# Token block sums: the sum of a quarter's high and low part made once a round and subtracted as one tile

## The chip, the cores and the metric

The kernel runs on one core of a Trainium2 chip. The metric is the device time of one execution in microseconds (us); the time of a kernel is the median of several executions.

## The reference

One decoder block on 1024 tokens of width 1024, all in float32, in two halves. What the change touches is the very front of it: the normed tokens `h` and their product with `w_in`.

```python
h = rmsnorm(x, g_mix_norm[l])
proj = jnp.einsum('bsd,de->bse', h, w_in[l])
sb_q, sb_k, sb_v, fx_q, fx_k, fx_v, f_logit, m_q, gate_logit = split_columns(proj, SPLITS)
# three attention branches (stick-breaking, forgetting, memory), gated and merged
mh = rmsnorm(mem, g_mem_norm[l])
mkv = jnp.einsum('bmd,de->bme', mh, w_mem_kv[l])
# ... x = x + merged @ w_out, then a squared-ReLU MLP with w_ff_up and w_ff_down
```

## The kernel before, in words

Every product is made on TensorE (PE) from a *high* part (rounded to a reduced 32-bit format, fp32r) and a *low* part (the rest) of both operands, three matmuls for one: high by high, high by low, low by high. So an operand that comes as one float32 tile has to be split: ScalarE (ACT) copies it to the high part, VectorE (DVE) subtracts this from the tile and writes the low part. Both steps stand in the helper `split`, and nearly all of them show in a profile as L1149 (ACT) and L1150 (DVE).

The large products are not made block by block but by a scheme with seven products, P1 to P7, for four blocks. P5, P6 and P7 need sums of blocks of the tokens. `h` turned, with its 1024 features on the partitions, lies in `hTh` (high) and `hTl` (low); a *quarter* is four chunks of 128 features by 512 tokens. The generator `sums_T` makes three sums out of three quarters, one chunk k a round, four rounds: with h11 the first quarter (it is kept only as high and low part, `b11`), t1 and t2 the same chunk of the two quarters of the second 512 tokens, which come back by DMA from a DRAM copy (`h_scr`) as float32,

- t1 = t1 - h11, the operand of P5
- t2 = t2 - t1, the operand of P6
- w_ = t2 - h11, the operand of P7

and each is then split into its place in `T_of` by `both`. Since h11 exists as two parts only, each subtraction of it takes two DVE instructions in a row, one for the high, one for the low part (L628 and L629, L635 and L636). L632 is t2 - t1. Those instructions run between 66.7 and 92.2 us of the profiled execution. The places t1, t2 and w_ are taken from a rotation `SN` of ten tiles of 128x512, which the first-stage evictions (L1328 on ACT, L1332 on DVE, values; L1753, gates) and the stores behind them use as well.

In the same stretch PE works through the first products: values of the forgetting branch (into `fn` go the forget logits, L1360), one gate block, then keys and values of the memory, `w_kv`. The weights of `w_kv` come in eight pieces of 512 KB through SP's DMA queue into two raw tiles, `ra` and `rb`, in turn, and are split into pairs of high and low tiles: (`ha`, `la`), (`hc`, `lc`), (`hb`, `lb`), again in turn. A piece's transfer can only be issued once the split of the piece before it in the same raw tile is over on DVE, and after whatever stands in front of it in SP's queue.

The order of the work is not the chip's choice. A planner inside the kernel (`Machine`) runs all generators against assumed costs (`dve_time` and the like), and each engine's instructions are written out in the order in which this plan begins them. On the chip every engine then takes its own queue strictly in that order. A changed cost or an instruction more or less can therefore move the order on every engine. All engines wait for each other by semaphores, and a tile out of a rotation can be written only after its last reader.

Of the kernel before, what the change touches and what calls it, by code (L numbers as in the profile page):

```python
# [18 lines left out]
ALU = mybir.AluOpType  # L19
# [19 lines left out]
def f32(ap):  # L39
    return ap.bitcast(F32)  # L40
# [3 lines left out]
def tile_hybrid_block(  # L44
# [23 lines left out]
    nc = tc.nc  # L68
# [120 lines left out]
    class Machine:  # L189
# [12 lines left out]
        def spawn(self, gen, late=0.0):  # L202

            done = Event()
            proc = [gen, late, done, None]
            self.at(self.now, lambda: self.resume(proc, None))
            return done
# [90 lines left out]
    def dve_time(*cols):  # L298
        return sum(0.08 + 0.00105 * m for m in cols)
# [60 lines left out]
    def tiles(pool, tag, n, shape, dt=F32):  # L360
        return Places([pool.t(tag, [P, shape], dt) for _ in range(n)])
# [3 lines left out]
    SN, RS, S1 = tiles(E, "sn", 10, 512), tiles(R, "raw", 4, 1024), R.t("s1", [P, 4, 256])  # L365
# [210 lines left out]
    def prologue():  # L576

        keys = [[("x", s)] for s in range(ST)] + [[("m", 0), ("m", 1)]]
        xs = [("x", s) for s in range(2, PLAIN)] + [(k_, s) for s in range(PLAIN, ST) for k_ in ("x", "xt")]
        spawn(fetch_tokens([("x", 0), ("g", "x"), ("x", 1), ("w", 0), ("w", 1), *xs[:1], ("g", "xt"), *xs[1:], ("g", "mt"),  # L580
                            *[(k_, s) for s in range(2) for k_ in ("m", "mt")]]))
        spawn(warm(half_made[2, 1]), 100.0)
        evs = [spawn(norm(ks_, 4.0 * i - 8.0, half_made[AFTER[i]] if i in AFTER else None), 4.0 * i - 8.0)
               for i, ks_ in enumerate(keys)]
        for ev in evs:
            yield ev
        spawn(small_loads())
        N.close()
        T = Pool("t", h=6)
        holder["T"] = T  # L590
        for kind in ("P5", "P6", "P7"):
            T_of[kind] = tuple(T.t("h", [P, 4, 512], F32R) for _ in range(2))
        spawn(sums_T(), 6.0)
# [10 lines left out]
    def second_half(k):  # L604

        t1, t2 = yield Get(SN, 2)

        def issue():
            nc.sync.dma_start(t1, h_scr[:, k, :])
            nc.sync.dma_start(t2, h_scr[:, 4 + k, :])  # L610
        yield from transfer(issue, 2 * P * 2048, 0.2)
        fetched_h[k] = t1, t2
    fetched_h = {}

    def sums_T():
        for s in range(4, ST):
            yield h_kept[s]
        coming = spawn(second_half(0))
        for k in range(4):
            b11 = tuple(t[:, k, 0:512] for t in (hTh, hTl))  # L620
            yield coming
            t1, t2 = fetched_h[k]
            if k < 3:
                coming = spawn(second_half(k + 1))
            w_ = yield Get(SN)

            def first():
                nc.vector.tensor_tensor(t1, t1, f32(b11[0]), ALU.subtract)  # L628
                nc.vector.tensor_tensor(t1, t1, f32(b11[1]), ALU.subtract)  # L629

            def second():
                nc.vector.tensor_tensor(t2, t2, t1, ALU.subtract)  # L632

            def third():
                nc.vector.tensor_tensor(w_, t2, f32(b11[0]), ALU.subtract)  # L635
                nc.vector.tensor_tensor(w_, w_, f32(b11[1]), ALU.subtract)  # L636
            yield Op("DVE", dve_time(512, 512), first)
            yield Op("DVE", dve_time(512), second)
            two = [spawn(both("P6", k, t2)), spawn(both("P5", k, t1), 2.0)]
            yield Op("DVE", dve_time(512, 512), third)  # L640
            two.append(spawn(both("P7", k, w_), 1.0))
            for ev in two:
                yield ev
            SN.put(t1, t2, w_)
        yield kv_over
        MT.close()
        holder["T4"] = T4 = Pool("t4", side="right", h=2)
        T_of["P4"] = tuple(T4.t("h", [P, 4, 512], F32R) for _ in range(2))
        for k in range(4):
            b21 = tuple(t[:, 4 + k, 0:512] for t in (hTh, hTl))  # L650
            t2 = tuple(t[:, k] for t in T_of["P6"])
            t4, w_ = yield Get(SN, 2)

            def fourth():
                nc.vector.tensor_tensor(t4, f32(b21[0]), f32(t2[0]), ALU.subtract)
                nc.vector.tensor_tensor(w_, f32(b21[1]), f32(t2[1]), ALU.subtract)
                nc.vector.tensor_tensor(t4, t4, w_, ALU.add)
            yield Op("DVE", dve_time(512, 512, 512), fourth)
            yield spawn(both("P4", k, t4))
            SN.put(t4, w_)  # L660

    def both(kind, k, raw):
        hi, lo = (t[:, k] for t in T_of[kind])
        yield from split(hi, lo, raw)
        machine.fire(T_made[kind][k])
# [1496 lines left out]
    with tc.manual_schedule():  # L2162
# [256 lines left out]
        def turn_half(s, k4):  # L2419
# [17 lines left out]
            if s >= 4:  # L2437
                yield turned[s - 4]
                if k4:
                    yield t1_made[s]  # L2440
                to = (t1raw, t2raw)[k4]

                def sums_T():
                    for h in range(2):
                        k2 = slice(2 * h, 2 * h + 2)
                        tt(to[h][:, :, cs], tr4[:, k2, :], t1raw[h][:, :, cs] if k4 else traw[:, k2, cs], ALU.subtract)
                yield Op("DVE", dve_time(256, 256), sums_T)
                if k4 == 0:
                    machine.fire(t1_made[s])
# [139 lines left out]
        first = {}  # L2589
# [266 lines left out]
```

## Time and profile before

| | us |
|---|---|
| median of 3 runs (lowest, highest) | 1657.71 (1656.91 to 1659.15) |
| the profiled execution's own time | 1657.59 |
| its span, from the first to the last instruction | 1655.8 |
| PE busy in the span | 1646.7 |
| DVE busy in the span | 1293.4 |
| ACT busy in the span | 849.5 |
| granted TensorE clock, mean | 0.999 |

Around the span lie 1657.59 - 1655.8 = 1.8 us. Of the views used below, the one of waits says which engine's instruction stood still for which other engine's, in total, how often, and the longest; the chain of waits goes back from the last instruction, at each step to what released it; the timeline gives start, duration and, in brackets, the idle time ahead of an instruction and its releaser; windows give busy time in a stretch. A matmul's end is modelled, so two matmuls' starts say more than their durations.

### The profile page before, as it was taken

What the parts mean: (1) busy time and instruction counts of PE and PEld (TensorE: products, weight loads), DVE (VectorE), ACT (ScalarE), POOL (GpSimd) and SP (SyncE); (2) the same over time, 40 slices, a digit from 0 to 9 for tenths busy, and PEclk for the clock granted to TensorE, in tenths of its full rate; (3) what the DMA queues carried; (4) which work ended last, traced back from release to release, by engine and by line L of the source; (5) the groups of instructions that cost most, each with busy time, mean ns of one, the idle gap of its engine ahead of it and who ended that gap; (6) DMA issues with size and microseconds to landing.
All of it is one profiled execution on the core that took longest, in us unless ns stands there. A gap on an engine that the chain in (4) does not pass through costs nothing.

```text
span 1655.8 us, 25062 instructions
## 1 busy us (share of the span) xinstructions
PE 1646.7 (99%) x9082; PEld 1429.4 (86%) x9082; DVE 1293.4 (78%) x2123; ACT 849.5 (51%) x1476; POOL 254.8 (15%) x440
## 2 busy tenths in 40 slices
PE   9999999999999999999999999999999999999999
PEld 8988899998888988888888888888888888888887
DVE  7798789955549888868877798987777777788875
ACT  6355555535458898977772465533233345233331
POOL 0000000000153232245400011021221120000000
PEclk9999999999999999999999999999999999999999
DMA  9846655568474455477866762154444475564532
GB/s 331 254 142 200 213 165 187 169 183 252 146 245 137 150 155 169 138 222 223 219 167 216 256 231 98 52 178 146 156 156 153 146 285 198 193 215 158 203 127 76
DMA packets 153629, 302.68 MB, mean 183 GB/s; under 512 B 18081, under 2 KB 58593, under 8 KB 153122
## 3 DMA queue, kind: packets, MB, share of 16 engines
q1 hardware_dynamic: 121970, 201.45, 36.2%
q0 software_dynamic: 31536, 99.64, 19.6%
q8 instruction: 71, 1.16, 0.3%
q14 instruction: 52, 0.43, 0.1%
HBM read 201.89 MB, written 99.13 MB: 182 GB/s over the span
## 4 chain that ended last, share of the span: by engine, by line
PE 94%; DVE 3%; DMA 2%; ACT 1%; issue 0%; SPq 0%
PE pp L1551 11%; PE pp L1239 9%; PE pp L2101 9%; PE pp L2791 8%; PE sc L1551 7%; PE sc L1239 6%; PE sc L2101 5%; PE tr L2791 4%; PE sc L2791 4%; PE tr L1012 4%; PE pv L1551 3%; PE pv L2791 3%; PE sc L1029 2%; PE tr L2101 2%; PE pp L1029 2%; PE pp L2346 2%
## 5 line engine op out<-in xcount | busy, mean ns | idle before, releaser
L1019 DVE TENSOR_TENSOR ptl<-tr,pth 128x512 fp32r<-128x512 f32 (+1 forms) x160 | 99.1, 628 | 25.5 <-ACT pth L1017 24.5
L2101 PE MATMUL pp<-h,oh 128*128 128x512 f32 x384 | 118.3, 389 | 0.0
L1017 ACT ACTIVATE pth<-tr 128x512 fp32r<-128x512 f32 (+1 forms) x160 | 87.5, 557 | 33.5 <-PE sc L1029 13.9
L2189 ACT ACTIVATE cu<-pp 128x512 f32<-128x512 f32 x48 | 28.7, 598 | 137.3 <-PE pp L2101 137.3
L2101 PEld LDWEIGHTS pp<-h,oh 128*128 128x128 f32 x384 | 72.0, 188 | 15.0 <-ACT oh L2532 0.2
L1468 POOL DMA_DIRECT2D raw<-w_in x32 | 24.2, 757 | 393.3 <-DVE lc L1150 205.2
L2101 PE MATMUL pp<-h,ol 128*128 128x512 f32 x192 | 74.9, 390 | 0.5 <-DVE ol L2037 0.5
L938 DVE TENSOR_TENSOR_SCAN e<-r,e 128x384 f32<-128x384 f32 (+3 forms) x64 | 66.3, 1044 | 6.8 <-ACT e L923 6.4
L2791 PE MATMUL pp<-h,h 128*128 128x512 f32 x288 | 66.6, 389 | 0.0
L2791 PE MATMUL pp<-sop,sop 128*128 128x512 f32 x288 | 66.6, 389 | 0.0
L2791 PEld LDWEIGHTS pp<-h,h 128*128 128x128 f32 x288 | 54.1, 188 | 11.2
L2791 PEld LDWEIGHTS pp<-sop,sop 128*128 128x128 f32 x288 | 54.1, 188 | 11.2
L1012 PE MATMUL tr<-ident,e 128*128 128x128 f32 x416 | 62.5, 273 | 0.0
L1012 PEld LDWEIGHTS tr<-ident,e 128*128 128x128 f32 x416 | 50.5, 140 | 9.9
L2118 POOL DMA_DIRECT2D s_scr<-cu x48 | 26.1, 544 | 189.3 <-DVE cu L2108 179.8
L1029 PE MATMUL sc<-pth,v 128*128 128x256 f32 (+1 forms) x174 | 48.0, 298 | 0.0
L2037 DVE TENSOR_TENSOR cu<-cu,sc 128x512 f32<-128x512 f32 x33 | 22.5, 682 | 32.5 <-ACT cu L2189 32.5
L1099 POOL DMA_DIRECT2D h<-sbk_scr x64 | 33.3, 527 | 94.1 <-PE pv L156 29.5
L2706 ACT ACTIVATE h<-t 128x2048 fp32r<-128x2048 f32 (+1 forms) x9 | 15.4, 1724 | 59.5 <-DVE t L2037 55.4
L2037 DVE TENSOR_TENSOR x<-x,pp 128x512 f32<-128x512 f32 x39 | 26.6, 683 | 22.8 <-PE pp L2791 22.8
L2101 PEld LDWEIGHTS pp<-h,ol 128*128 128x128 f32 x192 | 36.0, 188 | 8.7 <-DVE ol L2037 1.2
L2118 POOL DMA_DIRECT2D s_scr<-s x60 | 32.5, 542 | 71.0 <-DVE s L2037 64.4
(797 smaller groups left out, 5546.7 us busy)
## 6 DMA issues: line engine op xcount, KB each, us to landing
ur<-s_scr SPq DMA_DIRECT2D x26, 1024.0 KB
raw<-w_in POOLq DMA_DIRECT2D x32, 512.0 KB, 5.2
raw<-w_up SPq DMA_DIRECT2D x60, 256.0 KB
s_scr<-s POOLq DMA_DIRECT2D x60, 256.0 KB, 2.5
g<-w_down SPq DMA_DIRECT2D x14, 1024.0 KB
s_scr<-cu POOLq DMA_DIRECT2D x48, 256.0 KB, 2.3
h<-sbk_scr POOLq DMA_DIRECT2D x64, 128.0 KB, 3.1
o<-gate_scr SPq DMA_DIRECT2D x32, 256.0 KB
```

The source lines that it names most:

```text
L938: nc.vector.tensor_tensor_scan(out=back, data0=rho[:, :u][:, ::-1], data1=back, initial=0.0 if last else beta[:, c + u:c + u + 1], op0=ALU ...
L1012: nc.tensor.transpose(tr[:, jj * 256 + a * P:jj * 256 + (a + 1) * P], es[a][:, j * P:(j + 1) * P], ident)
L1017: yield Op("ACT", act_time(512 - lo_c), lambda: nc.scalar.activation(ph[:, lo_c:], tr[:, lo_c:], AF.Copy))
L1019: yield Op("DVE", dve_time(512 - lo_c), lambda: nc.vector.tensor_tensor(pl[:, lo_c:], tr[:, lo_c:], f32(ph[:, lo_c:]), ALU.subtract))
L1029: nc.tensor.matmul(pv[0][:, c_:256], pair.v[:, j, b, :], p_[:, jj * 256 + c_:(jj + 1) * 256], start=(k == 0 and n_ == 0 and i == 0), stop= ...
L1099: nc.gpsimd.dma_start(f32(t[k][rows_, :]), src)
L1239: nc.tensor.matmul(ps, a_, b_, start=(first and i == 0), stop=(last and i == n - 1))
L1551: nc.tensor.matmul(out_, a_, b_, start=(first and n == 0 and j == 0), stop=(last and n == 3 and j == len(todo) - 1), skip_group_check=True)
L2037: nc.vector.tensor_tensor(out_, a_, b_, op)
L2101: nc.tensor.matmul(ps, w[a_][:, k * P:(k + 1) * P], h[b_][k], start=(first and k == 0 and i == 0), stop=(last and k == 3 and i == 2), skip ...
L2118: nc.gpsimd.dma_start(s_scr[r0:r0 + P, :], t)
L2791: nc.tensor.matmul(ps, a_[:, c, qs], b_[:, c, :], start=(kind in ("P1", "P2", "P7") and c == 0 and i == 0), stop=(kind in ("P2", "P4", "P3 ...
```

## The change

In each round the two parts of h11 are added into w_ first, before the round waits for t1 and t2. Both subtractions of h11 then take w_ as one tile, and the last one writes over it. L622 is the new addition; L629, L632 and L635 are the three subtractions in the changed file. The planner is told of one DVE instruction instead of two at either place, and of the new one. The place w_ is taken ahead of the wait for t1 and t2 instead of behind it.

```diff
         for k in range(4):
             b11 = tuple(t[:, k, 0:512] for t in (hTh, hTl))
+            w_ = yield Get(SN)
+            yield Op("DVE", dve_time(512), lambda: nc.vector.tensor_tensor(w_, f32(b11[0]), f32(b11[1]), ALU.add))
             yield coming
             t1, t2 = fetched_h[k]
             if k < 3:
                 coming = spawn(second_half(k + 1))
-            w_ = yield Get(SN)
 
             def first():
-                nc.vector.tensor_tensor(t1, t1, f32(b11[0]), ALU.subtract)
-                nc.vector.tensor_tensor(t1, t1, f32(b11[1]), ALU.subtract)
+                nc.vector.tensor_tensor(t1, t1, w_, ALU.subtract)
 
             def second():
                 nc.vector.tensor_tensor(t2, t2, t1, ALU.subtract)
 
             def third():
-                nc.vector.tensor_tensor(w_, t2, f32(b11[0]), ALU.subtract)
-                nc.vector.tensor_tensor(w_, w_, f32(b11[1]), ALU.subtract)
-            yield Op("DVE", dve_time(512, 512), first)
+                nc.vector.tensor_tensor(w_, t2, w_, ALU.subtract)
+            yield Op("DVE", dve_time(512), first)
             yield Op("DVE", dve_time(512), second)
             two = [spawn(both("P6", k, t2)), spawn(both("P5", k, t1), 2.0)]
-            yield Op("DVE", dve_time(512, 512), third)
+            yield Op("DVE", dve_time(512), third)
             two.append(spawn(both("P7", k, w_), 1.0))
```

The order that results: PE (8750 rows), POOL and SP have the same instructions in the same order as before, apart from the numbers of the tiles they take out of the rotation. DVE has 2047 instead of 2051 rows, and DVE and ACT differ in order only within the four rounds of `sums_T`; from the split of the fourth `w_kv` piece on (`la` from `rb`, 93 to 96 us before) they agree again. In the changed file every line behind the edit has a number lower by one (L1150 is L1149 there). In the rows below, h_125 and h_129 are the high and low part of h11, h_905 to h_910 the operands of P5, P6 and P7 (high and low part of each), and sn tiles are the rotation's.

DVE, third and fourth round, before:

```order
L628 TENSOR_TENSOR sn_151<-sn_151,h_125 128x512
L629 TENSOR_TENSOR sn_151<-sn_151,h_129 128x512
L1150 TENSOR_TENSOR la_175<-ra_174,ha_173 128x1024
L1150 TENSOR_TENSOR lc_178<-rb_176,hc_177 128x1024
L632 TENSOR_TENSOR sn_152<-sn_152,sn_151 128x512
L635 TENSOR_TENSOR sn_149<-sn_152,h_125 128x512
L636 TENSOR_TENSOR sn_149<-sn_149,h_129 128x512
L1150 TENSOR_TENSOR h_908<-sn_152,h_907 128x512
L1150 TENSOR_TENSOR h_906<-sn_151,h_905 128x512
L1150 TENSOR_TENSOR h_910<-sn_149,h_909 128x512
L628 TENSOR_TENSOR sn_154<-sn_154,h_125 128x512
L629 TENSOR_TENSOR sn_154<-sn_154,h_129 128x512
```

DVE, the third round, now:

```order
L622 TENSOR_TENSOR sn_150<-h_125,h_129 128x512
L1359 COPY fn<-pp_140 128x8
L629 TENSOR_TENSOR sn_152<-sn_152,sn_150 128x512
L632 TENSOR_TENSOR sn_154<-sn_154,sn_152 128x512
L635 TENSOR_TENSOR sn_150<-sn_154,sn_150 128x512
L1149 TENSOR_TENSOR la_175<-ra_174,ha_173 128x1024
L1149 TENSOR_TENSOR h_908<-sn_154,h_907 128x512
L1149 TENSOR_TENSOR h_910<-sn_150,h_909 128x512
L1149 TENSOR_TENSOR h_906<-sn_152,h_905 128x512
L1149 TENSOR_TENSOR lc_178<-rb_176,hc_177 128x1024
```

The round's subtractions stood behind the splits of the first two `w_kv` pieces and stand ahead of both now; `lc` has moved behind the round's own three splits.

DVE, the end of the fourth round, before:

```order
L632 TENSOR_TENSOR sn_147<-sn_147,sn_154 128x512
L635 TENSOR_TENSOR sn_146<-sn_147,h_125 128x512
L636 TENSOR_TENSOR sn_146<-sn_146,h_129 128x512
L1150 TENSOR_TENSOR h_908<-sn_147,h_907 128x512
L1150 TENSOR_TENSOR h_906<-sn_154,h_905 128x512
L1150 TENSOR_TENSOR lb_180<-ra_174,hb_179 128x1024
L1150 TENSOR_TENSOR h_910<-sn_146,h_909 128x512
L1150 TENSOR_TENSOR la_175<-rb_176,ha_173 128x1024
```

and now:

```order
L622 TENSOR_TENSOR sn_155<-h_125,h_129 128x512
L629 TENSOR_TENSOR sn_148<-sn_148,sn_155 128x512
L632 TENSOR_TENSOR sn_147<-sn_147,sn_148 128x512
L635 TENSOR_TENSOR sn_155<-sn_147,sn_155 128x512
L1149 TENSOR_TENSOR h_908<-sn_147,h_907 128x512
L1149 TENSOR_TENSOR h_910<-sn_155,h_909 128x512
L1149 TENSOR_TENSOR h_906<-sn_148,h_905 128x512
L1149 TENSOR_TENSOR lb_180<-ra_174,hb_179 128x1024
L1149 TENSOR_TENSOR la_175<-rb_176,ha_173 128x1024
```

`lb`, the low part of the third `w_kv` piece, has one split more in front of it, and two subtractions less.

ACT, the splits of the third round and of the first two `w_kv` pieces, before:

```order
L1149 ACTIVATE ha_173<-ra_174 128x1024
L1149 ACTIVATE hc_177<-rb_176 128x1024
L1753 ACTIVATE sn_150<-pp_138 128x512
L1149 ACTIVATE h_907<-sn_152 128x512
L1149 ACTIVATE h_905<-sn_151 128x512
L1149 ACTIVATE h_909<-sn_149 128x512
L1753 ACTIVATE sn_155<-pp_139 128x512
```

and now:

```order
L1148 ACTIVATE ha_173<-ra_174 128x1024
L1148 ACTIVATE h_907<-sn_154 128x512
L1148 ACTIVATE h_909<-sn_150 128x512
L1148 ACTIVATE h_905<-sn_152 128x512
L1148 ACTIVATE hc_177<-rb_176 128x1024
L1752 ACTIVATE sn_151<-pp_138 128x512
L1752 ACTIVATE sn_146<-pp_139 128x512
```

The second piece's high part and the eviction of the first gate bank (which SP's queue stores, ahead of the transfers of the third and fourth piece) have moved behind the round's three splits.

## The prediction

> **What bounds the kernel now.** I read the page's busy shares and its chain first, to see which engine sets the end:
>
> ```profile
> span 1655.8 us, 25062 instructions
> ## 1 busy us (share of the span) xinstructions
> PE 1646.7 (99%) x9082; PEld 1429.4 (86%) x9082; DVE 1293.4 (78%) x2123; ACT 849.5 (51%) x1476; POOL 254.8 (15%) x440
> ...
> PE 94%; DVE 3%; DMA 2%; ACT 1%; issue 0%; SPq 0%
> ```
>
> PE is idle for only 1655.8 - 1646.7 = 9.1 us of the span, and the chain that ended last is PE for 94% of it. DVE work counts only where PE stands still for it. The second view is therefore PE's waits over the whole run, and beside it the two ends of the run in windows (PE busy is the second number):
>
> ```profile
> PE pp L1239 <- DVE lb L1150: 1.5, 2, 1.1
> PE pv L451 <- POOL ident masks.py:199: 1.4, 1, 1.4
> PE tr L547 <- DVE xt L500: 1.3, 1, 1.3
> PE pp L2101 <- DVE ol L2037: 0.5, 1, 0.5
> PE pp L1239 <- DVE h L553: 0.2, 1, 0.2
> PE pp L1239 <- DVE g L535: 0.2, 1, 0.2
> ```
>
> ```profile
> 0.00:50.00 50.00, 46.93 (x371) 45.55 (x372) 38.46 (x114) 31.92 (x62) 0.70 (x6) 1.00 0.98 326
> ...
> 1650.00:1656.00 6.00, 1.90 (x9) 1.25 (x7) 0.69 (x1) 0.00 (x0) 0.00 (x0) 0.83 0.23 87
> ```
>
> 3.1 us of idle time lie in the first 50 us and some 3.9 us behind the last matmul, and the change touches neither. What is left for it is the first row: two waits of PE for `lb`, the low part of a `w_kv` piece, 1.5 us in all. The third view, the chain between 75 and 95 us, says who made `lb` late:
>
> ```profile
> 75.31 7.15 DMA rb<-w_kv
> ...
> 82.48 1.07 ACT hc L1149
> ...
> 84.72 0.69 DVE sn L632
> ...
> 86.86 1.80 DVE h L1150 x3
> 88.66 0.61 DVE sn L628
> ...
> 89.30 0.70 DVE sn L629
> ...
> 90.03 0.70 DVE sn L632
> ...
> 92.09 1.28 DVE h L1150 x2
> 93.37 1.15 DVE lb L1150
> ...
> 94.56 1.70 PE pp L1239 x12
> ```
>
> This is the work that the change shortens: from 84.7 to 93.4 us DVE does nothing but the third and fourth round's sums and their splits, and `lb` queues behind them. The sums' own readers, the matmuls of the seven products in L1551, are nowhere among PE's waits.
>
> **What the stall costs.** PE's timeline: a transposition-to-matmul switch without a wait (the first two rows), then the place in question:
>
> ```profile
> 54.36 0.37 PE L1239 MATMUL pp<-hc,h 128*128 128x264 f32 x1
> 54.57 0.28 PE L1239 MATMUL pp<-lc,h 128*128 128x264 f32 x1
> ...
> 93.06 0.36 PE L1239 MATMUL pp<-hb,mt 128*128 128x256 f32 x1
> 94.56 0.39 PE L1239 MATMUL pp<-lb,mt 128*128 128x256 f32 x1 [1.14 <-DVE lb L1150]
> ...
> 95.98 0.28 PE L1239 MATMUL pp<-ha,mt 128*128 128x256 f32 x1
> 96.30 0.39 PE L1239 MATMUL pp<-la,mt 128*128 128x256 f32 x1
> 96.52 0.28 PE L1239 MATMUL pp<-ha,mt 128*128 128x256 f32 x1
> ...
> 103.16 0.39 PE L1239 MATMUL pp<-lb,mt 128*128 128x256 f32 x1 [0.41 <-DVE lb L1150]
> ```
>
> Undisturbed, `lb` would start 54.57 - 54.36 = 0.21 us behind the first `hb`, at 93.27. The matmuls then start 0.12 us apart (95.98 - 94.56 = 1.42 holds eleven steps, the first of them a slow one). Eleven steps bring `ha` at 94.59, `la` at 94.71 and the next `ha` at 94.83. It came at 96.52. So the first stall, with its restarts and the short gap ahead of `la`, costs 96.52 - 94.83 = 1.69 us of PE's time, though the view of waits shows only 1.14. I take 1.69, from starts. The Trainium skill bears on that choice: by "Perfetto Trace Analysis", section "Tensor Engine Instruction (MATMUL, LD_WEIGHTS)", the profiler computes a matmul's end from its size rather than observing it. The rows agree, durations of 0.28 at a spacing of 0.12. By the idle time alone the gain would be 1.1 us.
>
> The second stall, 0.41 at 103.16, is no part of the gain. There `hb` can be written only when PE has read its last content, and the ACT copy and DVE subtraction behind that take their 1.1 and 1.2 us whenever PE arrives; shifted as a whole, it stays.
>
> **The change part by part.** *Removed and added on DVE.* Per round two subtractions go that hang on their forerunner (starts 0.73 apart: 89.30, 90.03), and one addition comes that waits for nothing (0.60, as the three L1150 of 86.86, 1.80 in all) or has a follower that hangs on it (0.73). Four rounds: -8 x 0.73 + 4 x 0.60 to 0.73 = -3.4 to -2.9 us of DVE time. The first addition falls into idle time of DVE and the others into rounds that now have less to do. DVE as a whole is no bound, so none of this counts by itself.
>
> *Moved on ACT and SP.* This could cost. The rows of before that set it:
>
> ```profile
> 81.11 1.06 ACT L1149 ACTIVATE ha<-ra 128x1024 fp32r<-128x1024 f32 x1 [2.51 <-DMA ra<-w_kv]
> ...
> 85.44 1.15 ACT L1149 ACTIVATE h<-sn 128x512 fp32r<-128x512 f32 x2 [1.41 <-DVE sn L632]
> ...
> 87.43 0.60 ACT L1753 ACTIVATE sn<-pp 128x512 f32<-128x512 f32 x1
> ...
> 91.81 1.04 ACT L1149 ACTIVATE hb<-ra 128x1024 fp32r<-128x1024 f32 x1
> ```
>
> ```profile
> 84.06 0.32 SPq L1757 DMA_DIRECT2D gate_scr<-sn  x1
> 84.48 0.38 SPq L1157 DMA_DIRECT2D ra<-w_kv  x1
> 84.97 0.52 SPq L1157 DMA_DIRECT2D rb<-w_kv  x1
> ```
>
> `ha` keeps its 81.11, since it waits for a transfer. The third round's sums are over before it. Three splits at 0.57 then stand between `ha` and `hc`: `hc` starts at 81.11 + 1.0 + 3 x 0.57 = 83.8 instead of 82.48, the gate bank's eviction behind it is 1.3 late, and with it SP's queue: the store at 85.3, `ra` (third piece) at 85.75. `rb` (fourth) waits for `lc`: `la` at 82.2, 1.14, three low parts at 0.60, so `lc` from 85.15 to 86.4, and `rb` is issued at 86.4 instead of 84.97. PE's first `lc` matmul stands at 88.72: 2.3 us of cover, so the delay of `hc` and `lc` costs nothing by itself.
>
> *The fourth round.* On DVE, behind `lc`: addition 86.3, then 87.0, 87.7 and 88.45, over at 89.1. ACT has its second gate eviction at 87.43 as before (PE sets it), then three splits from 88.4 on, each waiting for its sum, until 90.3. `hb` can start at 90.3 instead of 91.81, `lb` runs from 91.35 to 92.6, `ha` until 92.4, `la` until 93.7. PE wants `lb` at 93.27 and `la` at 94.71. Both are early, by 0.7 and 1.0 us: the whole 1.69 us is gained, if the third piece has landed by 90.3 + 0.7 = 91.0.
>
> *The transfers.* No row names their landing, but the windows bound it (last number GB/s):
>
> ```profile
> 84.00:90.00 6.00, 6.00 (x39) 5.45 (x38) 5.89 (x9) 2.32 (x5) 0.00 (x0) 1.00 0.78 262
> 90.00:95.00 5.00, 3.86 (x32) 3.66 (x31) 4.91 (x7) 4.25 (x7) 0.00 (x0) 1.00 0.00 0
> ```
>
> Both pieces and two gate stores were in by 90.0. Issued 1.3 to 1.4 later, both are in by 91.4, the third piece ahead of the fourth. At the early end nothing is lost; at the late end `hb` starts at 91.4, `lb` is over at 93.7, PE stands 0.4 us, and the gain is 1.25. I take 1.69, since `ra` is first in the queue.
>
> *Behind it.* PE, POOL and SP keep their order, the later pieces hang on `lb` and `la` being over, which are 1.9 and 2.5 us earlier, and PE stood still for DVE only once more, 0.5 us in L2101. So the gain is carried to the end. **Sum:** 1657.59 - 1.7 = 1655.9 for an execution like the profiled one. The median was 0.12 above it: **1656.0**.
>
> **The rivals.** (a) *The late pieces eat the gain.* In the chain the second piece took 7.15 us. Were the third and fourth as slow, `rb` would land at 86.4 + 7.15 = 93.55, `ha` end at 94.6, `la` at 95.85, and PE's `la` start at 95.9 instead of 96.30: 0.4 gained, 1657.3. For it: two pieces and a store travel at once. Against: they did so before and were done in 5.5 us.
>
> (b) *Slower: the fifth piece.* It is issued once `lb` is over, now at 92.6. PE would come to `hc` 48 matmuls behind the first `hb`, at 94.83 + 34 x 0.12 = 98.9. If the piece takes 5.5 us, as the crowded ones, it lands at 98.1; copy and subtraction end it at 100.5; PE's `lc`, due at 99.05, stands 1.45 us, which leaves a gain of 0.2. At 7.15 us the stall is 3.1 and the run is 1.4 slower, 1659.1. It decides from about 5.7 us on. Against: the queues carried 0 GB/s from 90 to 95, and should again be empty by 91.4.
>
> (c) *The rotation.* Stores, loads and evictions get other `sn` tiles, and a writer could meet a reader that is not done, at a place where PE has no cover. The price is up to the chain's longest transfer, 7.15 us, so 1664 at most, and 1661 for half of it. Against: outside the rounds the order is the same on all engines, and the planner hands out no tile that is in use by its own plan.
>
> (d) *Nothing changes*: the time saved on DVE is spent waiting for ACT's splits, `lb` comes when it did, 1657.7. It needs ACT to stay at 91.81, and its forerunners say 90.3.
>
> **How the numbers follow.** Chances: forecast 0.66, (a) 0.13, (b) 0.08, (c) 0.05, (d) 0.08. The range, 1654.9 to 1658.4, takes the forecast with the scatter of three runs (lowest 0.8 below, highest 1.4 above the median), (a), (d) and the mild side of (b), and leaves out the bad side of (b) and (c). About 0.2% (3.3 us) is what a measurement of this kernel can tell from no change. A gain of 3.3 us would need idle time of PE that isn't there: 1.69 and 0.41 are all that the two stalls hold; 0.03 for something unseen. A loss of that size is (c) alone: 0.04. Within 0.2%: 0.93.
>
> **What would show it.** In the changed profile: the wait for `lb` near 94 us gone from PE's waits, the 0.41 left; `hb` on ACT near 90.4; SP's third piece issued near 85.7; PE's run behind 104 us earlier by 1.7. The step on transfers is wrong if ACT waits for `ra` ahead of `hb`; (b) holds if PE waits for `lc` near 99; (c) if a new wait shows behind 110 us. The forecast as a whole fails if PE's idle time falls and the span doesn't.

## The result and the profile after

The changed kernel took 1656.22 us (median of 22 runs, 1654.59 to 1658.82), the kernel before on the same chip 1658.95 us (22 runs, 1656.58 to 1661.29). The ratio is 0.9985, 95% interval 0.998 to 0.9991, so the change takes 1.5 to 3.3 us off. The interval keeps the gain clear of zero, and the ratio lies within the 0.2% that the prediction named as what a measurement can tell from no change. Forecast were 1656.0 us, and a gain of 1.7. That the absolute times agree to 0.2 us is partly luck: with more runs the kernel before stands 1.2 us above the median that the forecast started from.

The profiled execution has a span of 1653.8 us, 2.0 less than before. The page's span and busy times:

```profile
span 1653.8 us, 25062 instructions
PE 1646.2 (100%) x9082; PEld 1429.3 (86%) x9082; DVE 1290.8 (78%) x2119; ACT 849.5 (51%) x1476; POOL 254.8 (15%) x440
```

PE's busy time fell by 0.5 us, its idle time from 9.1 to 1653.8 - 1646.2 = 7.6 us. (A matmul behind a wait, or behind a switch from transpositions, is entered as longer, 0.36 to 0.39 us for 0.28, and so is part of a stall.) PE's waits, with their total, count and longest one:

```profile
PE pv L451 <- POOL ident masks.py:199: 1.4, 1, 1.4
PE tr L547 <- DVE xt L500: 0.9, 1, 0.9
PE pp L2100 <- DVE ol L2036: 0.5, 1, 0.5
...
```

The row for `lb` is gone, both waits of it. The timeline of PE for the stretch in question, first of before (the transpositions ahead of the third `w_kv` piece, and the first matmul of the seven products) and then of after:

```profile
92.92 0.38 PE L451 MATMUL pv<-ident 128*128 128x128 f32 x2
...
102.39 0.36 PE L1239 MATMUL pp<-hb,mt 128*128 128x256 f32 x1
...
103.39 0.40 PE L1239 MATMUL pp<-hb,mt 128*128 128x256 f32 x2
...
113.84 0.63 PE L1551 MATMUL pp<-h,hb 128*128 128x512 f32 x2
```

```profile
93.29 0.38 PE L451 MATMUL pv<-ident 128*128 128x128 f32 x2
93.43 0.36 PE L1238 MATMUL pp<-hb,mt 128*128 128x256 f32 x1
93.63 0.28 PE L1238 MATMUL pp<-lb,mt 128*128 128x256 f32 x1
...
101.06 0.36 PE L1238 MATMUL pp<-hb,mt 128*128 128x256 f32 x1
101.26 0.28 PE L1238 MATMUL pp<-lb,mt 128*128 128x256 f32 x1
101.38 0.40 PE L1238 MATMUL pp<-hb,mt 128*128 128x256 f32 x2
...
107.32 0.28 PE L1238 MATMUL pp<-hc,mt 128*128 128x256 f32 x1
107.75 0.39 PE L1238 MATMUL pp<-lc,mt 128*128 128x256 f32 x1
...
112.05 0.63 PE L1550 MATMUL pp<-h,hb 128*128 128x512 f32 x2
```

PE came to this stretch 0.37 us later than before (93.29 against 92.92), although none of PE's instructions ahead of it has moved. That is scatter: over the profiled executions of all the kernels below, this point lies between 92.76 and 93.42. From there on: the first `lb` follows its `hb` by 0.20 us instead of 1.50, the second by 0.20 instead of 0.77, and the seventh piece's `lc` follows its `hc` by 0.43, some 0.22 more than an undisturbed group. The stretch from the transpositions to the first matmul of L1551 (L1550 now) takes 112.05 - 93.29 = 18.76 us instead of 113.84 - 92.92 = 20.92, 2.16 less. Behind it the two traces keep a distance of 2.16 - 0.37 = 1.79 us until 734 us. Around there PE gains another 0.25, at a place that the edit doesn't touch, and 2.04 us, the 2.0 of the spans, remain to the end. So the stretch holds what the change itself can be shown to give. I use its length as a second measure below, since the first 50 us don't blur it. It splits at the second group of `hb` (102.39 and 101.06): before 9.47 + 11.45, now 7.77 + 10.99. So the first stall gave 1.70 and the rest of the stretch 0.46.

The instructions that set this, on DVE, ACT and SP, first three of before:

```profile
93.29 1.22 DVE L1150 TENSOR_TENSOR lb<-ra,hb 128x1024 fp32r<-128x1024 f32 x1
```

```profile
100.79 1.06 ACT L1149 ACTIVATE hb<-rb 128x1024 fp32r<-128x1024 f32 x1 [1.55 <-PE pp L1239]
```

```profile
96.28 0.37 SPq L1157 DMA_DIRECT2D rb<-w_kv  x1
```

and those after the change, on ACT, DVE and SP:

```profile
81.61 1.06 ACT L1148 ACTIVATE ha<-ra 128x1024 fp32r<-128x1024 f32 x1 [4.22 <-DMA ra<-w_kv]
84.14 1.04 ACT L1148 ACTIVATE hc<-rb 128x1024 fp32r<-128x1024 f32 x1
90.75 1.04 ACT L1148 ACTIVATE hb<-ra 128x1024 fp32r<-128x1024 f32 x1
96.57 1.06 ACT L1148 ACTIVATE hc<-ra 128x1024 fp32r<-128x1024 f32 x1 [0.94 <-DMA ra<-w_kv]
98.67 1.06 ACT L1148 ACTIVATE hb<-rb 128x1024 fp32r<-128x1024 f32 x1 [1.05 <-DMA rb<-w_kv]
```

```profile
82.71 1.23 DVE L1149 TENSOR_TENSOR la<-ra,ha 128x1024 fp32r<-128x1024 f32 x1 [1.58 <-ACT ha L1148]
91.83 1.23 DVE L1149 TENSOR_TENSOR lb<-ra,hb 128x1024 fp32r<-128x1024 f32 x1 [0.17 <-ACT hb L1148]
...
99.77 1.23 DVE L1149 TENSOR_TENSOR lb<-rb,hb 128x1024 fp32r<-128x1024 f32 x1 [0.28 <-ACT hb L1148]
```

```profile
86.13 0.38 SPq L1156 DMA_DIRECT2D ra<-w_kv  x1
86.91 0.38 SPq L1156 DMA_DIRECT2D rb<-w_kv  x1
...
94.45 0.37 SPq L1156 DMA_DIRECT2D rb<-w_kv  x1
```

The first piece came in 0.5 us later than before (`ha` 81.61, not 81.11), and still `hb` starts at 90.75 instead of 91.81 and `lb` at 91.83 instead of 93.29. The sixth piece's transfer (the last SP row) is issued at 94.45 instead of 96.28, and the second `hb` starts at 98.67 instead of 100.79.

### The profile page after: what moved, and what is told of

Same layout as the page of the kernel before. It is cut to its first block, busy times and chain, and to the rows that moved or that the text cites. A ratio compares the mean times of both kernels' runs of the same rounds, so it can differ in the third digit from the quotient of the medians.

```text
span 1653.8 us, 25062 instructions
## 1 busy us (share of the span) xinstructions
PE 1646.2 (100%) x9082; PEld 1429.3 (86%) x9082; DVE 1290.8 (78%) x2119; ACT 849.5 (51%) x1476; POOL 254.8 (15%) x440
## 4 chain that ended last, share of the span: by engine, by line
PE 95%; DVE 3%; DMA 1%; ACT 0%; issue 0%; SPq 0%
PE pp L1550 11%; PE pp L1238 10%; PE pp L2100 9%; PE pp L2790 8%; PE sc L1550 7%; PE sc L1238 6%; PE sc L2100 5%; PE tr L2790 4%; PE sc L2790 4%; PE tr L1011 4%; PE pv L1550 3%; PE pv L2790 3%; PE sc L1028 2%; PE tr L2100 2%; PE pp L1028 2%; PE pp L2345 2%
```

## The experiments

Theory L: the gain is what PE stood still for `lb`, and nothing else of the change counts. Its rivals are C (each DVE instruction saved counts by itself), O (it is the new order, not the smaller number of instructions) and T (the tiles that the rotation hands out, or the place taken early). A second question came with the result: what the second stall hung on.

| kernel | us against the kernel before (95%) | stretch, us | to the second `hb` | from there |
|---|---|---|---|---|
| before | | 20.92 | 9.47 | 11.45 |
| the change | -2.5 (-3.3 to -1.5) | 18.76 | 7.77 | 10.99 |
| count_only | -1.3 (-2.7 to 0.2) | 20.49 | 8.78 | 11.71 |
| order_only | -1.7 (-3.0 to -0.2) | 19.61 | 8.31 | 11.30 |
| place_early | -0.5 (-2.0 to 0.8) | 20.35 | 9.27 | 11.08 |
| fourth_plus2 | -1.8 (-3.3 to -0.5) | 19.74 | 8.37 | 11.37 |
| fourth_plus4 | 0.2 (-1.3 to 1.7) | 20.43 | 9.29 | 11.14 |
| second_plus2 | -2.5 (-3.8 to -1.0) | 18.73 | 7.75 | 10.98 |
| hold_fourth | 0.0 (-1.5 to 1.5) | 20.97 | 7.77 | 13.20 |
| pool_add | -0.2 (-1.7 to 1.3) | 20.21 | 8.77 | 11.44 |
| sixth_late | 0.0 (-1.5 to 1.3) | 20.52 | 8.61 | 11.91 |
| sixth_early | -0.5 (-2.0 to 1.0) | 19.75 | 8.49 | 11.26 |
| pool_ahead | -1.8 (-3.3 to -0.3) | 18.76 | 7.77 | 10.99 |

Microseconds are the ratio's distance from 1, and its interval's, times the median of the kernel before on that chip. The stretch is from one profiled execution of each kernel. In every row the change of the stretch lies within the interval of the times. The stretch scatters as well, with the landing of the transfers: `place_early`, which keeps the order of before, is 0.57 us shorter. The three kernels in which PE doesn't wait for `lb` or `lc` at all, or hardly (the change, `second_plus2`, `pool_ahead`), agree within 0.03 us, for there no landing matters. Since the intervals of the experiments are some 3 us wide, the times alone tell few of these kernels apart; most of what follows rests on the stretch and on PE's waits.

**The parts of the change.** `count_only` has the new arithmetic, but the addition stands in `first()` behind the wait, and the planner is told the old costs, so that DVE keeps its old order with four instructions less.

```diff
 def first():
-    nc.vector.tensor_tensor(t1, t1, f32(b11[0]), ALU.subtract)
-    nc.vector.tensor_tensor(t1, t1, f32(b11[1]), ALU.subtract)
+    nc.vector.tensor_tensor(w_, f32(b11[0]), f32(b11[1]), ALU.add)
+    nc.vector.tensor_tensor(t1, t1, w_, ALU.subtract)
```

> The change's arithmetic (one addition, three subtractions a round), with the planner told the old costs and the addition written directly ahead of the first subtraction, so that ACT, SP, POOL and PE keep the order of before, and DVE too apart from the four instructions that are gone. Theory L (the gain is PE's two waits for lb, and what counts is only how late lb is): two DVE instructions fewer, 1.44 us, stand between lc and lb; hb starts near 91.1 instead of 91.8 and lb is over near 93.4 where PE wants it at 93.3, so the first stall of 1.69 us shrinks to 0.3 to 0.5; the sixth piece is issued about 1.1 us earlier, and its stall stays at 0.4 to 0.6. Total 1.3 us faster than before (0.9 to 1.7), about half of the change's 2.4. Rival C (the DVE time saved is the gain, whatever the order): as fast as the change, 2.4 faster. Rival O (the new order is the gain): no faster than before.

Measured: 1657.13 us, ratio 0.9992 (0.9984 to 1.0001). PE still waited for `lb` twice:

```profile
PE pp L1238 <- DVE lb L1149: 1.1, 2, 0.6
```

`order_only` turns it round: the old arithmetic in the change's order, the planner being told of an addition that isn't there.

```diff
-yield Op("DVE", dve_time(512), lambda: nc.vector.tensor_tensor(w_, f32(b11[0]), f32(b11[1]), ALU.add))
+yield Op("DVE", dve_time(512), lambda: None)
 ...
-    nc.vector.tensor_tensor(t1, t1, w_, ALU.subtract)
+    nc.vector.tensor_tensor(t1, t1, f32(b11[0]), ALU.subtract)
+    nc.vector.tensor_tensor(t1, t1, f32(b11[1]), ALU.subtract)
```

> The arithmetic of before (two subtractions each time, five DVE instructions a round), with the planner told what the change tells it, so that every engine has the order of the change and DVE one instruction more a round. Theory L: the third round's extra instruction falls into DVE's wait for ha ahead of la (1.58 us in the changed profile); the fourth's makes lb 0.72 late, which the 0.5 us of cover at PE's first lb nearly takes: a first stall of 0.2 to 0.4, a second of 0.2 to 0.3. Total 1.7 us faster than before (1.3 to 2.1). Rival C: no faster than before. Rival O: 2.4 faster, as the change.

Measured: 1657.03 us, 0.999 (0.9982 to 0.9999), no wait for `lb` but a new one for the seventh piece's `lc`, the third row of its view of waits:

```profile
PE pp L1240 <- DVE lc L1151: 0.4, 1, 0.4
```

`place_early` is the kernel before with only the place w_ taken ahead of the wait.

> Before, with the one edit that w_'s place in the rotation is taken ahead of the wait for t1 and t2. The order of all engines is that of before; only the numbers of the rotation's tiles are others. Theory L: no change, within 0.5 us, and PE's two waits for lb stay at 1.5 us in all. Rival T (the gain comes from the other tiles of the rotation, which free a store or a load earlier): up to 2.4 us faster.

Measured: 1658.56 us, 0.9997 (0.9988 to 1.0005), as expected. T's full 2.4 us lie outside the interval, and in the profile `lb` comes 12.20 us behind `ha`, where it was 12.18 before. So T falls.

By the stretch, the order alone gives 1.31 us, the count alone 0.43, both 2.16. That the order matters more is not shown by this, for the first piece landed 11.5 us ahead of PE's transpositions in `count_only`'s profile and 12.1 in `order_only`'s (11.8 before). What leaves the landing out is the way from the start of `ha` on ACT to the start of `lb` on DVE, first of `count_only`, then of `order_only`:

```profile
81.82 1.06 ACT L1148 ACTIVATE ha<-ra 128x1024 fp32r<-128x1024 f32 x1 [3.03 <-DMA ra<-w_kv]
```

```profile
92.95 1.23 DVE L1149 TENSOR_TENSOR lb<-ra,hb 128x1024 fp32r<-128x1024 f32 x1 [0.18 <-ACT hb L1148]
```

```profile
81.03 1.06 ACT L1150 ACTIVATE ha<-ra 128x1024 fp32r<-128x1024 f32 x1 [3.25 <-DMA ra<-w_kv]
```

```profile
92.32 1.23 DVE L1151 TENSOR_TENSOR lb<-ra,hb 128x1024 fp32r<-128x1024 f32 x1 [0.17 <-ACT hb L1150]
```

It is 93.29 - 81.11 = 12.18 us before, 11.13 in `count_only`, 11.29 in `order_only` and 91.83 - 81.61 = 10.22 in the change. So the count alone brings `lb` forward by 1.05 us, the order alone by 0.89, and the change by 1.96, about their sum: the two parts count about equally. Both do the same thing. `lb` begins at the landing of the *first* piece plus the DVE work that stands behind that wait; the count makes this work less, and the order puts all of the third round's subtractions ahead of `la`, where DVE has time until the first piece is there.

**More and less DVE work, in the right place and in the wrong one.** Two or four instructions that change nothing (a maximum of w_ with itself, 0.7 us each) are put into the change's fourth round, behind the wait for the first piece and ahead of `lb`, or (`k == 1`) into its second round, which is over before that wait. The diff is that of `fourth_plus2`.

```diff
     nc.vector.tensor_tensor(w_, t2, w_, ALU.subtract)
+    if k == 3:
+        for _ in range(2):
+            nc.vector.tensor_tensor(w_, w_, w_, ALU.max)
```

> The change, with two more DVE instructions of 0.7 us behind the last subtraction of the fourth round (the maximum of w_ and itself, which leaves it as it is); the order is otherwise the change's. Theory L: lb is 1.44 us later than in the change and has 0.5 us of cover: PE waits for lb some 0.9 us and loses 1.1 to 1.3 us against the change, so the run is 1.2 us faster than before. Rival O (order alone): as fast as the change, 2.4 faster than before.

> As the run with two more DVE instructions in the fourth round, but four. Theory L: lb 2.9 us later than in the change, of which 0.5 to 1.0 is covered: PE's first wait for lb 1.5 to 2.2 us, a second of about 0.3; the gain is gone, 0.2 us faster than before (0.8 faster to 0.4 slower). Rival O (order alone): 2.4 faster, as the change.

> The change, with the two more DVE instructions of 0.7 us in the second round instead of the fourth. Theory L: they end ahead of la, for which DVE waits 1.1 to 1.6 us anyway (ha waits for a transfer), so lb is as early as in the change: no wait of PE for lb, 2.4 us faster than before (1.9 to 2.6). Rival C (DVE time is what counts, wherever it lies): as with the two in the fourth round, 1.2 to 1.8 faster, with PE waiting for lb.

Measured: 1656.85 us, 0.9989 (0.998 to 0.9997); 1658.58 us, 1.0001 (0.9992 to 1.001), the gain gone; 1655.67 us, 0.9985 (0.9977 to 0.9994), the whole gain kept with 1.4 us more of DVE work than the change. The stretch reads 19.74, 20.43 and 18.73. So L gets its dose: by the stretch, the same two instructions cost nothing in the second round (18.73, no wait for `lb`) and 19.74 - 18.76 = 0.98 us in the fourth. C had both alike, with a wait for `lb` in `second_plus2`, and falls by this, though the times of these two runs overlap. O falls with `fourth_plus4`, which has the change's order and none of its gain. By the times `fourth_plus2` came out some 0.6 us better than expected, well within its interval; by the stretch (20.92 - 19.74 = 1.18) it is what was expected. In `second_plus2` the first piece landed 0.8 us earlier ahead of PE than in the change, and the added work reached some half microsecond past that landing, so the test is a little kinder than planned.

**Two other ways to an early `lb`, both misses.** `hold_fourth` is the kernel before with the fourth round's sums held back by 10 us in the plan, so that the splits of the later pieces go first.

```diff
+            if k == 3:
+                yield Sleep(10.0)
             yield Op("DVE", dve_time(512, 512), first)
```

> The arithmetic of before, all its twenty sums, with the one edit that the planner holds the fourth round back for 10 us of its own time, so that lb and la of the third and fourth w_kv piece stand ahead of it on DVE and ACT. Theory L: hb starts at 88 to 89, lb is over by 91, 2 us ahead of PE; the fifth and sixth piece are issued 3 us earlier than before. No wait of PE for lb is left: 2.4 us faster than before (1.9 to 2.7), without any instruction saved. Rival C (the DVE time saved is the gain): no faster than before. Rival O (the change's order on ACT and SP is the gain): no faster either, since the third round keeps the order of before.

Measured: 1658.22 us, 1.0 (0.9991 to 1.0009). `lb` began at 90.01 and PE didn't wait for it, as expected; the way to the second `hb` is 7.77 us, exactly the change's. But the sums now lie between the splits of the later pieces, and the plan has another order there. PE's longest wait behind 105 us, and DVE's rows ahead of it:

```profile
109.56 0.39 PE L1241 MATMUL pp<-lc,mt 128*128 128x256 f32 x1 [1.49 <-DVE lc L1152]
```

```profile
105.42 1.22 DVE L1483 TENSOR_TENSOR s<-raw,raw 128x1024 f32<-128x1024 f32 x1
106.55 0.69 DVE L821 TENSOR_TENSOR sn<-sn,st 128x512 f32<-128x512 f32 x1
107.16 1.22 DVE L1483 TENSOR_TENSOR raw<-raw,raw 128x1024 f32<-128x1024 f32 x1
108.29 1.22 DVE L1152 TENSOR_TENSOR lc<-rb,hc 128x1024 fp32r<-128x1024 f32 x1
```

The high part `hc` was there at 106.04 (ACT from 104.98, 1.06), and DVE took the seventh piece's `lc` only at 108.29, with no idle time ahead. In the kernel before, `lc` waited for its `hc`, and the second of the sums of weight blocks (L1483 here, L1481 there) stood behind it:

```profile
108.26 1.22 DVE L1150 TENSOR_TENSOR lc<-rb,hc 128x1024 fp32r<-128x1024 f32 x1 [0.15 <-ACT hc L1149]
109.40 1.22 DVE L1481 TENSOR_TENSOR raw<-raw,raw 128x1024 f32<-128x1024 f32 x1
```

So 1.70 us were gained on the way to the second `hb`, and 13.20 - 11.45 = 1.75 net given back behind it. My expectation had looked at the wait to be removed, and not at how the order behind it would move.

`pool_add` puts the four additions on GpSimd, which leaves DVE four instructions less than the change has.

```diff
-yield Op("DVE", dve_time(512), lambda: nc.vector.tensor_tensor(w_, f32(b11[0]), f32(b11[1]), ALU.add))
+yield Op("POOL", 1.5, lambda: nc.gpsimd.tensor_tensor(w_, f32(b11[0]), f32(b11[1]), ALU.add))
```

> The change, with the four additions made on GpSimd instead of DVE, so that DVE has another 2.4 to 2.9 us less to do; the planner puts la and lc of the first two w_kv pieces ahead of the third round's sums again. Theory L: lb is over by 92.6, ahead of PE, so there is no wait for it, and nothing more to win than in the change: 2.4 us faster than before (1.9 to 2.7). Rival C: twice the DVE time saved, 4 to 5 faster.

Measured: 1658.0 us, 0.9999 (0.999 to 1.0008), and PE waited for `lb` twice. With this cost the planner puts the splits of the first two pieces ahead of the third round's sums again, and a store ahead of that round's two loads on SP. The first piece's transfer, which stands behind them, was issued at 76.91 instead of 75.22, and DVE stood still for it longer than in any other kernel here:

```profile
76.91 0.43 SPq L1156 DMA_DIRECT2D ra<-w_kv  x1
```

```profile
83.77 1.23 DVE L1149 TENSOR_TENSOR la<-ra,ha 128x1024 fp32r<-128x1024 f32 x1 [3.86 <-ACT ha L1148]
...
93.08 1.23 DVE L1149 TENSOR_TENSOR lb<-ra,hb 128x1024 fp32r<-128x1024 f32 x1 [0.18 <-ACT hb L1148]
```

From `ha` (82.68) to `lb` it is 10.40 us, near the change's 10.22, but `ha` began only 10.74 us ahead of PE's transpositions instead of 11.68. So 0.94 of the 1.12 us by which `lb` was later than in the change, as PE sees it, came with the late landing and 0.18 from the work behind it.

Two explanations stood: the order, or GpSimd itself. `pool_ahead` is the same kernel with 0.6 instead of 1.5 told to the planner, which gives the change's order on PE, DVE and SP, and on ACT too, but for one eviction of 128x512 that has changed places with the instruction behind it.

> The change with the four additions on GpSimd instead of DVE, as in pool_add, but with a smaller cost told to the planner, so that DVE, ACT and SP keep the change's order exactly (third round's sums ahead of the split of the first w_kv piece), and DVE has four instructions less. Theory L with the order (the wait for the first piece has to be covered by the sums; DVE time saved ahead of that wait is worth nothing): no wait of PE for lb, as the change, 2.4 below the kernel before [1.9 to 2.9], and DVE idle for some 2.5 us ahead of la near 82. Theory P (GpSimd's additions themselves cost, by slowing DVE or being late): 0.5 below, as pool_add. Theory C (each DVE instruction counts by itself): 2.4 + 4 x 0.6 = 4.8 below.

Measured: 1655.95 us, 0.9989 (0.998 to 0.9998), stretch 18.76, the change's. So it was the order (on SP too, where the first piece was issued at 75.55), C falls a second time (4.8 us were its price, outside the interval), and GpSimd's part costs nothing on the path. One detail missed: DVE did not stand idle for 2.5 us ahead of `la`, for reasons told at the end.

**What the second stall hung on.** My prediction had it hang on PE's release of `hb` (R); the trace of after spoke for the sixth piece's transfer (D). `sixth_late` is the change, with one DVE instruction more that holds the raw tile of the fourth piece, and so the issue of the sixth:

```diff
         yield from split(pair[0][:, :kk * n], pair[1][:, :kk * n], raw[:, :kk * n])
+        state["pieces"] = state.get("pieces", 0) + 1
+        if state["pieces"] == 10:
+            yield Op("DVE", 0.0, lambda: nc.vector.tensor_tensor(raw[:, :1024], raw[:, :1024], raw[:, :1024], ALU.max))
         RAW.put(raw)
```

> The change, and one more DVE instruction, a maximum of the fourth w_kv piece's raw tile with itself (128x1024, some 1.2 us), behind that piece's split. It reads no other tile and only holds the raw tile back, so that SP issues the sixth piece's transfer near 95.7 instead of 94.45. The output is not changed. Theory D (the second stall hangs on the sixth piece's transfer): ACT's second hb starts near 99.9 instead of 98.67 and waits for the transfer, the second lb on DVE near 101.0, PE stands 0.8 to 1.1 us for it near 102.2, and loses some 1.2 us by starts: 1.2 [0.7 to 1.7] below the kernel before instead of 2.4. Theory R (my prediction's: the second stall hangs on PE's release of hb, and a later transfer is covered): no wait of PE for lb, 2.4 below.

Measured: 1657.77 us, 1.0 (0.9991 to 1.0008). The issue on SP, the second `hb` on ACT, and PE's two waits:

```profile
95.92 0.37 SPq L1156 DMA_DIRECT2D rb<-w_kv  x1
```

```profile
100.26 1.06 ACT L1148 ACTIVATE hb<-rb 128x1024 fp32r<-128x1024 f32 x1 [4.10 <-DMA rb<-w_kv]
```

```profile
101.37 0.39 PE L1241 MATMUL pp<-hb,mt 128*128 128x256 f32 x1 [0.60 <-ACT hb L1148]
102.63 0.39 PE L1241 MATMUL pp<-lb,mt 128*128 128x256 f32 x1 [0.87 <-DVE lb L1149]
```

The transfer was 1.47 us later than in the change and ACT's copy 1.59. R had no loss, 2.4 below the kernel before, and the interval excludes it. D is right in kind and somewhat small in size: PE came late already to `hb`, not only to `lb`, and the stretch lost 1.76 us (0.84 ahead of the second `hb`, 0.92 behind it) instead of some 1.2.

`sixth_early` moves the other way, in the kernel before: the fourth round's last split goes behind the fourth piece's, so that its raw tile comes free earlier.

```diff
+            if k == 3:
+                yield Sleep(2.0)
             two.append(spawn(both("P7", k, w_), 1.0))
```

> The kernel before, with the last split of the fourth round (the operand of P7) put behind the split of the fourth w_kv piece on DVE and ACT; nothing else changes its place. So la of the fourth piece is over 0.6 us earlier, and SP issues the sixth piece near 95.7 instead of 96.28, while lb of the third piece stays where it was. Theory D: PE's first wait for lb stays at 0.9 to 1.2 us, the second (0.41) falls to 0.1 or goes, ACT's second hb starts near 100.2: 0.6 below the kernel before [0 to 1.2]. Theory R: both waits as before, 0 [-0.5 to 0.5], ACT's second hb at 100.8.

Measured: 1657.68 us, 0.9997 (0.9988 to 1.0006). The time can't tell D from R here, and the profile is only half a test, since in this execution the first piece landed early and the first stall shrank (PE waited 0.37 us for `lb`) along with the second. What it does show is the distance from the sixth piece's issue (95.14) to ACT's copy (99.72), 4.58 us. Over all kernels that distance agrees with D. It is 4.51 before, 4.22 in the change, 4.72, 4.51, 4.14, 4.72, 4.52, 4.42, 4.42, 4.34 and 4.58 in the kernels in which ACT waited for the transfer, whenever it was issued between 93.99 and 96.35. In `hold_fourth` and `pool_ahead` (issued at 94.04 and 94.17) the profile names PE, and the distance is 3.63 and 3.65, so there the transfer had landed by then. Why it was quicker than in `second_plus2`, issued at 93.99 with 4.42, is open. In these two ACT's copy began 0.37 and 0.39 us behind the start of PE's last matmul that reads the old `hb` (97.30 to 97.67, and 97.43 to 97.82). In the kernel before that matmul started at 99.04, and the copy at 100.79, 1.75 later. There the profile named PE too, but PE had long been done; the distance from the issue, 4.51, is that of a copy that waited for its transfer.

## Why the prediction was right, and where it was not

*What bounds the kernel.* Right. Busy DVE time was of no account: minus four instructions on top of the change (`pool_ahead`) and plus two (`second_plus2`) leave the gain where it was.

*The first stall, 1.69 us.* Right, by its mechanism and its size: the way from the transpositions to the second `hb` is 9.47 - 7.77 = 1.70 us shorter. By the idle time that the view of waits shows it would have been 1.14. This is where the Trainium skill's "Perfetto Trace Analysis", section "Tensor Engine Instruction (MATMUL, LD_WEIGHTS)", was leaned on, by which a matmul's end is modelled: starts were the right thing to count, and the trace's 1.70 agrees with the forecast's 1.69 to 0.01 us.

*The steps on ACT, DVE and SP.* Right, once the first piece's later landing (0.50 us in this execution) is added to each: `hc` 83.8 + 0.5, measured 84.14; the third piece's issue 85.75 + 0.5, measured 86.13; the fourth's 86.4 + 0.5, measured 86.91; `hb` 90.3 + 0.5, measured 90.75; `lb` 91.35 + 0.5, measured 91.83. The transfers were in time, with no wait of ACT for the third piece. But these half microseconds are also the weak point: the cover of 0.7 us is of the size of the scatter of the landing, which lay between 10.7 and 12.8 us ahead of PE's transpositions over the profiled executions. So a part of the stall may be left in some executions; the one profile of the changed kernel shows none.

*The second stall: "shifted as a whole, it stays".* Wrong, and this is the step that failed. It rested on the bracket in the profile of before, which names PE as ACT's releaser at 100.79. The transfer decided, as `sixth_late` shows and the distances agree. It is issued once `la` of the fourth piece is over, and since the change brings `la` forward by 1.8 us, the copy came 2.1 us earlier while PE came only 1.33 earlier. So the second `lb` followed its `hb` by 0.20 instead of 0.77, and the `hb` after that by 0.32 instead of 1.00: 0.68 us more than predicted. The trace of before held the hint. Its windows (the last number is GB/s) and PE's last reader of the old `hb`:

```profile
99.50:100.00 0.50, 0.50 (x7) 0.50 (x6) 0.50 (x1) 0.00 (x0) 0.00 (x0) 1.00 0.34 107
100.00:100.50 0.50, 0.50 (x7) 0.50 (x6) 0.50 (x2) 0.00 (x0) 0.00 (x0) 1.00 0.05 18
```

```profile
99.04 0.28 PE L1239 MATMUL pp<-hb,mt 128*128 128x256 f32 x1
```

The transfers ended shortly behind 100.0, ahead of the copy at 100.79, and PE's reader had started 1 us before that.

*"So the gain is carried to the end".* Nearly: 0.22 us was given back at the seventh piece's `lc`, which DVE took at 106.48 though its `hc` was there at 105.97. This wait was in no step. The sum by its own terms is therefore 1.70 + 0.68 - 0.22 = 2.16 us, the 2.16 of the stretch, and the times say 2.5 (1.5 to 3.3). The 1.69 was short by a fifth of that.

*The rivals.* (a), late pieces, and (b), the fifth piece: neither happened; ACT had the fifth piece at 96.57, and PE didn't wait for its `lc`. (c), the rotation: nothing of it in PE's waits, and `place_early` shows none beyond its interval (its bound of 1664 is a slip, since 1657.6 + 7.15 is 1664.7). (d), `lb` comes when it did: not in the change, where it came 1.46 us earlier. The nearest to it is `pool_add`, where what was saved on DVE went into a longer wait for the first piece.

## What to carry to other kernels

In this kernel, DVE time saved was worth something only behind the next wait for data: an instruction less ahead of a transfer that hasn't landed only makes the engine wait longer (and two more there cost nothing), while moving independent work ahead of that wait gained nearly as much here as removing instructions behind it (0.89 and 1.05 us). When a trace names a releaser, look whether it had been done for long; here the gap between PE's last reader and ACT's copy (1.75 us, and 0.39 where PE did decide) told that a DMA was meant, and with it whether a second stall goes or stays. And ask of each wait that you remove by moving work how the order behind it and ahead of it will change; the same gain was lost once to the seventh piece's split, and once to a first piece that was issued 1.7 us later.

## What the runs showed of the hardware

With the additions on GpSimd, single DVE subtractions took twice their time. From `pool_ahead`, two of GpSimd's additions and the DVE subtractions that ran into them:

```profile
68.90 1.57 POOL L622 TENSOR_TENSOR sn<-h,h 128x512 f32<-128x512 f32 x1 [35.63 <-DMA v_fx<-sn]
...
77.82 1.67 POOL L622 TENSOR_TENSOR sn<-h,h 128x512 f32<-128x512 f32 x1 [4.83 <-DVE h L1149]
```

```profile
69.42 1.60 DVE L635 TENSOR_TENSOR sn<-sn,sn 128x512 f32<-128x512 f32 x1
...
78.67 1.38 DVE L629 TENSOR_TENSOR sn<-sn,sn 128x512 f32<-128x512 f32 x1
80.08 0.69 DVE L632 TENSOR_TENSOR sn<-sn,sn 128x512 f32<-128x512 f32 x1
```

The two took 1.60 and 1.38 us where the next one takes 0.69, and both ended 0.55 to 0.56 us after GpSimd's addition did (70.47 and 79.49, against 71.02 and 80.05), as if they had begun only then. The Trainium skill's "SBUF — State Buffer", section "Who interferes with whom", has a rule for it: a DVE instruction with two SBUF inputs contends with a GpSimd instruction that reads SBUF, and the one that comes second is blocked until the first is over. The rows agree. It is also part of why DVE had no idle time ahead of `la` in that kernel, where 2.5 us had been expected: 0.7 us went into the longer subtraction of the third round. Another 1.1 us are gone because `ha` began earlier than in the change, at 80.51 instead of 81.61.

The landing of a 512 KB piece scattered: 4.1 to 4.7 us from issue to the copy that waited for it at one place of the program, and `ha` of the first piece at 80.01 to 81.82 us (82.68 in `pool_add`, which issued it late). Half a microsecond of cover ahead of a transfer is not safe here.
